# RMS norm with swish on one core: register work gathered at the top of the loops, a scratch transfer left out, and three loads cut in two

## The chip, the cores and the metric

The kernel runs on one core of a Trainium2 chip. The metric is the device time of one execution in microseconds. Before the change it is 160.35 us, the median of three runs (160.17 to 160.7).

## The reference

The input x is 16 x 1024 rows of 512 float32 numbers (33.55 MB), gamma has 512 numbers and eps is 1e-5. Every row is normalised by its own root mean square, multiplied by gamma and put through swish:

```python
rms = np.sqrt(np.mean(x ** 2, axis=-1, keepdims=True) + eps)
x_norm = x / rms * gamma
return x_norm * (1.0 / (1.0 + np.exp(-x_norm)))
```

The output has the same shape and type as x, so 33.55 MB are read from HBM and 33.55 MB are written.

## The kernel before

**Tiling.** The 16384 rows are spread over 128 partitions, 128 rows to a partition. A "row" below is one such index: 128 rows of x at once, one on each partition, 2 KB on each, 256 KB together. The rows lie in four groups (32, 48, 16 and 32 of them); within a group each partition's rows are contiguous in HBM, so a transfer of n rows is one run of n x 2 KB on each partition. In SBUF they lie in `xb`, a ring of 96 places, worked on in place; row 96 takes the place of row 0.

**Transfers.** All large transfers are issued by SP, into one queue, in the order of the list `order` (lines 33 to 36). `loads` (line 30) cuts the 128 rows into 11 loads and `stores` (line 32) into 6 stores. SP first issues the loads up to row 79. It then waits until the load of rows 48 to 74 has landed, waits for the first 8 units and issues the store of rows 0 to 31 ("store 0"), the load of rows 80 to 95, waits until store 0 is done (its ring places are then free), issues the loads of rows 96 to 121 and 122 to 127, waits until the first of these two has landed, and issues the other five stores, each when the rows that it covers are finished (`s_swish`, line 122). The first two loads (`early = 2`) are put into the entry block ahead of SP's first drain (lines 145 to 154), so that they go out before the barrier with which the program begins. At the end SP waits for the scratch transfer (line 164) and for the stores.

**Compute.** Work goes in units of `cn = 4` rows, 32 units in all. For a unit, ACT squares three of the rows and sums them (`square`, line 206), DVE does the fourth (`sums`, line 244), POOL adds eps and takes the power -0.5 (`rsqrt`, line 182), DVE multiplies the four rows by that and by gamma (`norm`, line 251), and ACT applies Silu to the unit's 2048 numbers per partition (`swish`, line 215). PE only waits for each load and raises `s_land` by the units that it completes. ACT begins with two units written out, then a loop of 10 rounds of three units, then two swishes; DVE and POOL have loops of the same ten rounds. In ACT's and DVE's loops the place in the ring is kept in registers, and every unit adds 4 to it, takes it modulo 96 and works out an address for each row that it touches (lines 235 to 240 and 272 to 277, with `rows_of` and `row_of`).

**Small transfers.** ACT's queue carries two: `scratch`, 128 x 16 zeros written from SBUF to an HBM tensor that nothing reads (line 219), and gamma, read to four partitions (line 223) and spread by DVE to all.

Of the kernel before, what the change touches and what calls it, by code (L numbers as in the profile page):

```python
# [9 lines left out]
def kernel(  # L10
# [7 lines left out]
    nc = tc.nc  # L18
    P = nc.NUM_PARTITIONS
    AF = mybir.ActivationFunctionType  # L20
    ALU = mybir.AluOpType
    fp32 = mybir.dt.float32

    xf = x.flatten_outer_dims()
    of = out.flatten_outer_dims()
    R, D = xf.shape

    groups = [32, 48, 16, 32]
    ring = 96
    loads = [(0, 4), (4, 4), (8, 8), (16, 8), (24, 8), (32, 16), (48, 27), (75, 5)]  # L30
    loads += [(80, 16), (96, 26), (122, 6)]
    stores = [(0, 32), (32, 32), (64, 16), (80, 16), (96, 24), (120, 8)]
    order = [("load", a) for a in (0, 4, 8, 16, 24, 32, 48, 75)]
    order += [("landed", 48), ("store", 0), ("load", 80)]
    order += [("stored", 0), ("load", 96), ("load", 122)]
    order += [("landed", 96)] + [("store", a) for a in (32, 64, 80, 96, 120)]
    early = 2
    cn = 4

# [11 lines left out]
    U = 3  # L51
    rounds = (K - 2) // U
    assert U * rounds == K - 2
    load_at = {a: t for t, (a, _) in enumerate(loads)}
# [9 lines left out]
    def sbuf(name, shape, dt=fp32):  # L64
        return nc.alloc_sbuf_tensor(name, shape, dt).ap()

    xb = sbuf("xb", [P, ring, D])
# [9 lines left out]

    ld = [nc.alloc_semaphore(f"ld{t}") for t in range(len(loads))]
    st = [nc.alloc_semaphore(f"st{t}") for t in range(len(stores))]
    scratch = nc.dram_tensor("scratch", [P, 16], fp32, kind="Internal").ap()  # L80
    blank = sbuf("blank", [P, 16])
    s_blank = nc.alloc_semaphore("s_blank")
    s_scratch = nc.alloc_semaphore("s_scratch")
    s_gld = nc.alloc_semaphore("s_gld")
    s_zero = nc.alloc_semaphore("s_zero")
    s_half = nc.alloc_semaphore("s_half")
# [1 line left out]
    s_land = nc.alloc_semaphore("s_land")  # L88
# [7 lines left out]
    def need(ins, sem, value):  # L96
        return ins.wait_op(sem, value, "sem-ge")

    def take(queue, sem):
        queue.wait_ge(sem, 1).then_inc(sem, -1)  # L100

    def dram(ap, piece):
        a, n = piece
        g = max(g for g in range(len(groups)) if first[g] <= a)
        r = a - first[g]
        assert r + n <= groups[g], piece
        rows = ap[P * first[g] : P * (first[g] + groups[g])]
        return rows.rearrange("(p n) d -> p n d", n=groups[g])[:, r : r + n, :]

    def buf(piece):  # L110
        a, n = piece
        at = a % ring
        assert at + n <= ring, piece
        return xb[:, at : at + n, :]

    def load(t):
        return nc.sync.dma_start(
            out=buf(loads[t]), in_=dram(xf, loads[t])
        ).then_inc(ld[t], 16)

    def store(t):
        need(
            nc.sync.dma_start(out=dram(of, stores[t]), in_=buf(stores[t])),
            s_swish, ends[t],
        ).then_inc(st[t], 16)
# [17 lines left out]
    entry = nc.main_func.blocks[0].instructions  # L143
    here = nc.cur_bb.bb.instructions
    for t in range(early):
        ins = load(t).ins
        assert here[-1] is ins or here[-1].name == ins.name
        here.pop()
        at = next(
            i for i, other in enumerate(entry)  # L150
            if other.engine == mybir.EngineType.SP
            and isinstance(other, mybir.InstDrain)
        )
        entry.insert(at, ins)
    for what, a in order[early:]:
        if what == "load":
            load(load_at[a])
        elif what == "store":
            store(store_at[a])
        elif what == "landed":  # L160
            nc.sync.wait_ge(ld[load_at[a]], 16)
        else:
            nc.sync.wait_ge(st[store_at[a]], 16)
    nc.sync.wait_ge(s_scratch, 16)
    waited = {a for what, a in order if what == "stored"}
    for t, (a, _) in enumerate(stores):
        if a not in waited:
# [2 lines left out]
    passed = 0  # L170
    for t, (a, n) in enumerate(loads):
        units = (a + n) // cn
        nc.tensor.wait_ge(ld[t], 16).then_inc(s_land, units - passed)
        passed = units
    assert passed == K

    nc.gpsimd.memset(blank, 0.0).then_inc(s_blank, 1)  # L177
    nc.gpsimd.memset(gamma4, 0.0).then_inc(s_zero, 1)  # L178
    nc.gpsimd.memset(neg_half, -0.5).then_inc(s_half, 1)  # L179
    nc.gpsimd.wait_ge(s_half, 1)  # L180
# [14 lines left out]
        for j in range(U):  # L195
            rsqrt((2 + j) % U)

    def rows_of(queue, v, j, n=1):
        return xb[:, bass.ds(queue.snap(v + j, min_val=0, max_val=ring - n), n), :]

    def row_of(queue, v, j):
        if isinstance(v, int):
            return xb[:, v + j, :]
        return rows_of(queue, v, j).rearrange("p n d -> p (n d)")

    def square(u, rows):
        take(nc.scalar, s_land)
        for j in range(cn - 1):
            acc = nc.scalar.activation(  # L209
                out=junk[u * (cn - 1) + j], in_=rows[j], func=AF.Square,  # L210
                scale=inv_d**0.5, accum_out=ms[u][:, j : j + 1],
            )
        acc.then_inc(s_acc, 1)

    def swish(rows):
        take(nc.scalar, s_norm)
        nc.scalar.activation(out=rows, in_=rows, func=AF.Silu).then_inc(s_swish, 1)  # L217

    need(nc.scalar.dma_start(out=scratch, in_=blank), s_blank, 1).then_inc(
        s_scratch, 16  # L220
    )
    need(
        nc.scalar.dma_start(out=gamma4[0:P:32, :], in_=gamma.partition_broadcast(4)),
        s_zero, 1,
    ).then_inc(s_gld, 16)
    nc.scalar.preload_act_table_set("silu_and_others")  # L226
    at = [nc.scalar.alloc_register(f"at{j}") for j in range(U)]
    nc.scalar.reg_mov(at[1], 0)
    nc.scalar.reg_mov(at[2], cn)
    for k in range(2):  # L230
        square(k, [xb[:, k * cn + j, :] for j in range(cn)])
    with nc.scalar.Fori(0, rounds, 1):
        for j in range(U):
            now, old = at[j], at[(j + 1) % U]
            nc.scalar.reg_alu(now, at[(j + 2) % U], cn, op=ALU.add)
            nc.scalar.reg_alu(now, now, ring, op=ALU.mod)
            v = nc.scalar.snap(now, min_val=0, max_val=ring - cn)
            square((2 + j) % U, [row_of(nc.scalar, v, i) for i in range(cn)])
            w = nc.scalar.snap(old, min_val=0, max_val=ring - cn)
            swish(xb[:, bass.ds(w, cn), :])  # L240
    for k in range(K - 2, K):
        swish(buf((k * cn, cn)))

    def sums(u, row):
        take(nc.vector, s_acc)
        nc.vector.scalar_tensor_tensor(  # L246
            out=junk_v[u], in0=row, scalar=inv_d, in1=row,
            op0=ALU.mult, op1=ALU.mult, accum_out=ms[u][:, cn - 1 : cn],
        ).then_inc(s_sum, 1)

    def norm(u, rows):
        take(nc.vector, s_rstd)
        for j in range(cn):
            ins = nc.vector.scalar_tensor_tensor(  # L254
                out=rows[j], in0=rows[j], scalar=rstd[u][:, j : j + 1],
                in1=gamma_sb, op0=ALU.mult, op1=ALU.mult,
            )
        ins.then_inc(s_norm, 1)

    to = [nc.vector.alloc_register(f"to{j}") for j in range(U)]  # L260
    nc.vector.reg_mov(to[2], cn)
    sums(0, xb[:, cn - 1, :])
    need(nc.vector.stream_shuffle(gamma_sb, gamma4, [0] * 32), s_gld, 16).then_inc(  # L263
        s_gamma, 1
# [1 line left out]
    sums(1, xb[:, 2 * cn - 1, :])  # L266
    nc.vector.wait_ge(s_gamma, 1)
    norm(0, [xb[:, j, :] for j in range(cn)])
    with nc.vector.Fori(0, rounds, 1):
        for j in range(U):  # L270
            now, old = to[j], to[(j + 2) % U]
            nc.vector.reg_alu(now, old, cn, op=ALU.add)
            nc.vector.reg_alu(now, now, ring, op=ALU.mod)
            v = nc.vector.snap(now, min_val=0, max_val=ring - cn)
            sums((2 + j) % U, row_of(nc.vector, v, cn - 1))
            w = nc.vector.snap(old, min_val=0, max_val=ring - cn)
            norm((1 + j) % U, [row_of(nc.vector, w, i) for i in range(cn)])
    norm((K - 1) % U, [buf(((K - 1) * cn + j, 1))[:, 0, :] for j in range(cn)])


# [33 lines left out]
```

## Time and profile before

| | before |
|---|---|
| median of 3 runs | 160.35 us (160.17 to 160.7) |
| the profiled execution's own time | 159.91 us |
| its span | 158.6 us |
| bytes moved | 67.14 MB, 423 GB/s over the span |
| DMA queue q1 (SP's transfers) | 98.7% of 16 engines' span |
| ACT, DVE, POOL busy | 121.1, 107.9, 59.3 us |
| last store issued | 133.5 us |

The profile shows one execution. Its shares are busy time over the span. The DMA rows count packets, megabytes and the packets' time as a share of sixteen DMA engines over the span; a share can pass 100% in a short window, because a packet's time is counted where it starts. q1 is SP's queue, q10 ACT's, q14 carries instructions. In the rows of windows the columns are the stretch, its length, busy time of DVE, ACT and POOL with instruction counts, the clock of TensorE (not used here), the DMA engines' share and GB/s. The trace also records for each DMA packet its queue, start, duration and bytes, but not its engine. A transfer over 128 partitions is 128 packets, eight for each engine, and each engine ends its part with a 4-byte packet, called a completion mark here; the wait for a transfer ends when all sixteen are there. Packets of one engine follow each other so closely that they can be laid end to end, and in that way followed by engine.

### The profile page before, as it was taken

To read this page: it belongs to the slowest core of one execution; us is meant where nothing else is said; L and a number is where in the kernel's file an instruction comes from. 1 tells how busy PE (TensorE), PEld (TensorE's weight loads), DVE (VectorE), ACT (ScalarE), POOL (GpSimd) and SP (SyncE) were. 2 spreads that over 40 slices of the span, in tenths; PEclk is the share of its full clock that TensorE was granted. 3 is DMA by queue.
4 is the path that set the end of the run, shared out by engine and by line. 5 is a ranking of instruction groups with operands and counts; after the bars stand their busy time and mean duration, and the time that the engine had idled before them with its cause. 6 is when DMAs were issued, how large, how long until landed. Compare 5 with 4: busy or idle time off the path is not lost. (4 is left out here: it accounts for less than half of the span.)

```text
span 158.6 us, 1330 instructions
## 1 busy us (share of the span) xinstructions
DVE 107.9 (68%) x194; ACT 121.1 (76%) x225; POOL 59.3 (37%) x71
## 2 busy tenths in 40 slices
DVE  0119798888888888888888887989898991000000
ACT  0836999999999999999999999999999954000000
POOL 2034445555455555554444444444454530000000
DMA  7999999999969969979999999996989999999976
GB/s 267 433 428 438 430 481 432 482 446 432 446 300 546 496 298 512 463 314 421 405 430 430 430 430 410 516 512 281 529 380 405 405 504 405 479 397 397 508 343 273
DMA packets 2602, 67.14 MB, mean 423 GB/s; under 512 B 420, under 2 KB 420, under 8 KB 424
## 3 DMA queue, kind: packets, MB, share of 16 engines
q1 hardware_dynamic: 2448, 67.11, 98.7%
q10 hardware_dynamic: 152, 0.02, 0.1%
q14 instruction: 2, 0.02, 0.0%
HBM read 33.56 MB, written 33.56 MB: 423 GB/s over the span
## 5 line engine op out<-in xcount | busy, mean ns | idle before, releaser
L254 DVE SCALAR_TENSOR_TENSOR xb<-xb,rstd,gamma_sb 128x512 f32 (+1 forms) x128 | 87.5, 747 | 0.1
L217 ACT ACTIVATE xb<-xb (+1 forms) x32 | 61.1, 1908 | 4.8 <-ACTq L100 4.2
L209 ACT ACTIVATE junk<-xb 128x512 f32 (+1 forms) x96 | 56.1, 585 | 4.0 <-ACTq L100 3.9
L188 POOL TENSOR_TENSOR rstd<-aeps,neg_half 128x4 f32<-128x4 f32 x32 | 40.9, 1279 | 5.9 <-POOLq L100 5.9
L184 POOL TENSOR_SCALAR aeps<-ms 128x4 f32<-128x4 f32 x32 | 17.6, 550 | 61.5 <-POOLq L100 61.5
L246 DVE SCALAR_TENSOR_TENSOR junk_v<-xb 128x512 f32 (+1 forms) x32 | 22.1, 692 | 20.1 <-DVEq L100 20.1
L209 ACT ACTIVATION_READ_ACCUMULATOR junk<-xb 128x1 f32 x96 | 17.9, 186 | 0.0
L226 ACT ACT_TABLE_LOAD x1 | 1.3, 1283 | 3.7 <-issue 3.7
L246 DVE DVE_READ_ACCUMULATOR junk_v<-xb 128x1 f32 x32 | 2.7, 83 | 0.0
L263 DVE LOAD_MASK_SELECT gamma_sb<-gamma x1 | 0.0, 14 | 3.4 <-DMA gamma<-in_gamma_dram 3.4
L263 DVE STREAM_SHUFFLE gamma_sb<-gamma 128x512 f32<-128x512 f32 x1 | 0.7, 719 | 0.0
L177 POOL MEMSET blank<- 128x16 f32 x1 | 0.1, 111 | 1.5 <-POOLq L62 1.5
L178 POOL MEMSET gamma<- 128x512 f32 x1 | 0.5, 524 | 0.0
L295 POOL MEMSET const-float32-0.0<- 128x1 f32 x1 | 0.1, 98 | 0.2 <-issue 0.2
L295 POOL MEMSET const-uint8-127<- 128x1 uint8 x1 | 0.1, 103 | 0.0
L295 POOL MEMSET const-bfloat16-1.0<- 128x1 bf16 x1 | 0.1, 101 | 0.0
L179 POOL MEMSET neg_half<- 128x4 f32 x1 | 0.1, 101 | 0.0
L295 POOL MEMSET const-float32-1.0<- 128x1 f32 x1 | 0.1, 98 | 0.0
## 6 DMA issues: line engine op xcount, KB each, us to landing
xb<-in_x_dram SPq DMA_DIRECT2D x2, 4096.0 KB, 30.4
out_dram<-xb SPq DMA_DIRECT2D x2, 4096.0 KB, 33.5
xb<-in_x_dram SPq DMA_DIRECT2D x1, 6912.0 KB, 44.7
xb<-in_x_dram SPq DMA_DIRECT2D x1, 6656.0 KB, 25.4
xb<-in_x_dram SPq DMA_DIRECT2D x3, 2048.0 KB, 14.7
out_dram<-xb SPq DMA_DIRECT2D x1, 6144.0 KB, 26.4
xb<-in_x_dram SPq DMA_DIRECT2D x2, 1024.0 KB, 5.8
out_dram<-xb SPq DMA_DIRECT2D x1, 2048.0 KB, 25.0
```

What stands on the lines that cost most here:

```text
L177: nc.gpsimd.memset(blank, 0.0).then_inc(s_blank, 1)
L178: nc.gpsimd.memset(gamma4, 0.0).then_inc(s_zero, 1)
L179: nc.gpsimd.memset(neg_half, -0.5).then_inc(s_half, 1)
L184: nc.gpsimd.tensor_scalar(out=aeps[u], in0=ms[u], scalar1=eps_f, scalar2=None, op0=ALU.add,).then_inc(s_eps, 1)
L188: nc.gpsimd.tensor_tensor(out=rstd[u], in0=aeps[u], in1=neg_half, op=ALU.pow).then_inc(s_rstd, 1)
L209: acc = nc.scalar.activation(out=junk[u * (cn - 1) + j], in_=rows[j], func=AF.Square, scale=inv_d**0.5, accum_out=ms[u][:, j : j + 1],)
L217: nc.scalar.activation(out=rows, in_=rows, func=AF.Silu).then_inc(s_swish, 1)
L226: nc.scalar.preload_act_table_set("silu_and_others")
L246: nc.vector.scalar_tensor_tensor(out=junk_v[u], in0=row, scalar=inv_d, in1=row, op0=ALU.mult, op1=ALU.mult, accum_out=ms[u][:, cn - 1 : cn ...
L254: ins = nc.vector.scalar_tensor_tensor(out=rows[j], in0=rows[j], scalar=rstd[u][:, j : j + 1], in1=gamma_sb, op0=ALU.mult, op1=ALU.mult,)
L263: need(nc.vector.stream_shuffle(gamma_sb, gamma4, [0] * 32), s_gld, 16).then_inc(s_gamma, 1)
L295: nc = _bacc.Bacc("TRN2", target_bir_lowering=False, num_devices=1)
```

## The change

- ACT's and DVE's loops count units instead of rounds. At the top of each round `addresses` works out the addresses that the round needs (twelve on ACT, thirteen on DVE) from the loop's counter; the registers for the place in the ring, with their additions, modulos and copies per unit, are gone.
- The scratch transfer, the memset of its source, its two semaphores and SP's final wait are gone.
- The load of rows 48 to 74 becomes two, of 16 and 11 rows; the load of rows 96 to 121 becomes two, of 16 and 10. The two waits for a landed load now name the second pieces (rows 64 and 112).
- The first load (rows 0 to 3) goes out as two transfers on one semaphore: partitions 0 to 15, then 16 to 127. Both, and the second load, lie in the entry block ahead of SP's first drain.

```diff
-    loads = [(0, 4), (4, 4), (8, 8), (16, 8), (24, 8), (32, 16), (48, 27), (75, 5)]
-    loads += [(80, 16), (96, 26), (122, 6)]
+    loads = [(0, 4), (4, 4), (8, 8), (16, 8), (24, 8), (32, 16), (48, 16), (64, 11), (75, 5)]
+    loads += [(80, 16), (96, 16), (112, 10), (122, 6)]
-    order = [("load", a) for a in (0, 4, 8, 16, 24, 32, 48, 75)]
-    order += [("landed", 48), ("store", 0), ("load", 80)]
-    order += [("stored", 0), ("load", 96), ("load", 122)]
-    order += [("landed", 96)] + [("store", a) for a in (32, 64, 80, 96, 120)]
+    order = [("load", a) for a in (0, 4, 8, 16, 24, 32, 48, 64, 75)]
+    order += [("landed", 64), ("store", 0), ("load", 80)]
+    order += [("stored", 0), ("load", 96), ("load", 112), ("load", 122)]
+    order += [("landed", 112)] + [("store", a) for a in (32, 64, 80, 96, 120)]
...
+    parts = [[slice(0, P)] for _ in loads]
+    parts[0] = [slice(0, 16), slice(16, P)]
+    full = [16 * len(p) for p in parts]
+
     def load(t):
-        return nc.sync.dma_start(
-            out=buf(loads[t]), in_=dram(xf, loads[t])
-        ).then_inc(ld[t], 16)
+        return [
+            nc.sync.dma_start(
+                out=buf(loads[t])[part], in_=dram(xf, loads[t])[part]
+            ).then_inc(ld[t], 16)
+            for part in parts[t]
+        ]
...
-    nc.sync.wait_ge(s_scratch, 16)
...
-    nc.gpsimd.memset(blank, 0.0).then_inc(s_blank, 1)
...
+    slots = ring // cn
+    units = xb.rearrange("p (u n) d -> p u (n d)", n=cn)
+
+    def unit_of(i):
+        return units[:, bass.ds(i % slots, 1), :].rearrange("p u e -> p (u e)")
+
+    def row_of(unit, r):
+        return unit[:, r * D : (r + 1) * D]
+
+    def addresses(queue, aps):
+        for ap in aps:
+            queue.lower_ap(ap)
...
-    need(nc.scalar.dma_start(out=scratch, in_=blank), s_blank, 1).then_inc(
-        s_scratch, 16
-    )
...
-    with nc.scalar.Fori(0, rounds, 1):
+    with nc.scalar.Fori(0, rounds * U, U) as i:
+        new = [unit_of(i + j + 2) for j in range(U)]
+        old = [unit_of(i), unit_of(i + 1), new[0]]
+        sq_rows = [[row_of(unit, r) for r in range(cn - 1)] for unit in new]
+        addresses(nc.scalar, old + sum(sq_rows, []))
         for j in range(U):
-            now, old = at[j], at[(j + 1) % U]
-            nc.scalar.reg_alu(now, at[(j + 2) % U], cn, op=ALU.add)
-            nc.scalar.reg_alu(now, now, ring, op=ALU.mod)
-            v = nc.scalar.snap(now, min_val=0, max_val=ring - cn)
-            square((2 + j) % U, [row_of(nc.scalar, v, i) for i in range(cn)])
-            w = nc.scalar.snap(old, min_val=0, max_val=ring - cn)
-            swish(xb[:, bass.ds(w, cn), :])
+            square((2 + j) % U, sq_rows[j])
+            swish(old[j])
...
-    with nc.vector.Fori(0, rounds, 1):
+    with nc.vector.Fori(0, rounds * U, U) as i:
+        of_unit = [unit_of(i + j + 1) for j in range(U + 1)]
+        rows = [[row_of(unit, r) for r in range(cn)] for unit in of_unit]
+        addresses(nc.vector, sum(rows[:U], []) + rows[U][cn - 1 :])
         for j in range(U):
-            now, old = to[j], to[(j + 2) % U]
-            nc.vector.reg_alu(now, old, cn, op=ALU.add)
-            nc.vector.reg_alu(now, now, ring, op=ALU.mod)
-            v = nc.vector.snap(now, min_val=0, max_val=ring - cn)
-            sums((2 + j) % U, row_of(nc.vector, v, cn - 1))
-            w = nc.vector.snap(old, min_val=0, max_val=ring - cn)
-            norm((1 + j) % U, [row_of(nc.vector, w, i) for i in range(cn)])
+            sums((2 + j) % U, rows[j + 1][cn - 1])
+            norm((1 + j) % U, rows[j])
```

More of the change, by code (lines that the diff above doesn't have):

```diff
@@ L79 @@
     st = [nc.alloc_semaphore(f"st{t}") for t in range(len(stores))]
[L80 to L83, printed above, removed]
     s_gld = nc.alloc_semaphore("s_gld")
@@ L145 @@
     for t in range(early):
-        ins = load(t).ins
-        assert here[-1] is ins or here[-1].name == ins.name
-        here.pop()
+        moved = [piece.ins for piece in load(t)]
+        for ins in reversed(moved):
+            assert here[-1] is ins or here[-1].name == ins.name
+            here.pop()
         at = next(
@@ L153 @@
         )
-        entry.insert(at, ins)
+        for ins in reversed(moved):
+            entry.insert(at, ins)
     for what, a in order[early:]:
@@ L160 @@
         elif what == "landed":
-            nc.sync.wait_ge(ld[load_at[a]], 16)
+            nc.sync.wait_ge(ld[load_at[a]], full[load_at[a]])
         else:
             nc.sync.wait_ge(st[store_at[a]], 16)
-    nc.sync.wait_ge(s_scratch, 16)
     waited = {a for what, a in order if what == "stored"}
@@ L172 @@
         units = (a + n) // cn
-        nc.tensor.wait_ge(ld[t], 16).then_inc(s_land, units - passed)
+        nc.tensor.wait_ge(ld[t], full[t]).then_inc(s_land, units - passed)
         passed = units
     assert passed == K
-    nc.gpsimd.memset(blank, 0.0).then_inc(s_blank, 1)
     nc.gpsimd.memset(gamma4, 0.0).then_inc(s_zero, 1)
@@ L196 @@
             rsqrt((2 + j) % U)
[L198 to L204, printed above, removed]
+    slots = ring // cn
[7 more added lines that the diff above has]
+            queue.lower_ap(ap)
     def square(u, rows):
@@ L226 @@
     nc.scalar.preload_act_table_set("silu_and_others")
-    at = [nc.scalar.alloc_register(f"at{j}") for j in range(U)]
-    nc.scalar.reg_mov(at[1], 0)
-    nc.scalar.reg_mov(at[2], cn)
     for k in range(2):
         square(k, [xb[:, k * cn + j, :] for j in range(cn)])
-    with nc.scalar.Fori(0, rounds, 1):
-        for j in range(U):
-            now, old = at[j], at[(j + 1) % U]
-            nc.scalar.reg_alu(now, at[(j + 2) % U], cn, op=ALU.add)
-            nc.scalar.reg_alu(now, now, ring, op=ALU.mod)
-            v = nc.scalar.snap(now, min_val=0, max_val=ring - cn)
-            square((2 + j) % U, [row_of(nc.scalar, v, i) for i in range(cn)])
-            w = nc.scalar.snap(old, min_val=0, max_val=ring - cn)
-            swish(xb[:, bass.ds(w, cn), :])
+    with nc.scalar.Fori(0, rounds * U, U) as i:
[3 more added lines that the diff above has]
+        addresses(nc.scalar, old + sum(sq_rows, []))
+        for j in range(U):
+            square((2 + j) % U, sq_rows[j])
+            swish(old[j])
     for k in range(K - 2, K):
-        swish(buf((k * cn, cn)))
+        swish(units[:, k % slots, :])
     def sums(u, row):
@@ L258, in norm @@
         ins.then_inc(s_norm, 1)
-    to = [nc.vector.alloc_register(f"to{j}") for j in range(U)]
-    nc.vector.reg_mov(to[2], cn)
     sums(0, xb[:, cn - 1, :])
```

## The prediction

> **What bounds the kernel now.** I read the page's shares first, then the DMA queues, then SP's waits, then the DMA in narrow windows.
>
> ```profile
> span 158.6 us, 1330 instructions
> DVE 107.9 (68%) x194; ACT 121.1 (76%) x225; POOL 59.3 (37%) x71
> DMA  7999999999969969979999999996989999999976
> q1 hardware_dynamic: 2448, 67.11, 98.7%
> q10 hardware_dynamic: 152, 0.02, 0.1%
> q14 instruction: 2, 0.02, 0.0%
> ```
>
> The reader is to see a DMA-bound kernel: SP's queue (q1) fills 98.7% of what sixteen DMA engines have, and no compute engine passes 76%. q14 counts two packets of instructions; they matter below.
>
> ```profile
> SPq L161 <- DMA xb<-in_x_dram: 68.4, 2, 43.8
> SPq L123 <- ACT xb L217: 35.3, 3, 22.3
> SPq L117 <- DMA out_dram<-xb: 21.6, 1, 21.6
> ```
>
> These are SP's own waits, for landed loads, for finished swishes and for the one store that frees ring rows. They would cost time only if the DMA engines ran dry. In the packet records (start, duration, bytes of each) they never do: laid end to end the packets make sixteen unbroken rows from 1.04 to 158.07 us, with no gap above 0.13 us other than two of 0.30 us named below. Compute ends at 133.5 us and the stores then drain until 158, so compute is about 20 us off the path.
>
> ```profile
> 0.00:1.00 1.00, 0.00 (x0) 0.00 (x0) 0.19 (x4) 1.00 0.00 0
> 1.00:1.40 0.40, 0.00 (x0) 0.00 (x0) 0.00 (x0) 1.00 1.47 266
> 1.40:1.80 0.40, 0.00 (x0) 0.00 (x0) 0.00 (x0) 1.00 0.44 143
> 1.80:2.20 0.40, 0.00 (x0) 0.00 (x0) 0.28 (x2) 1.00 0.88 348
> 3.00:4.00 1.00, 0.00 (x0) 0.33 (x1) 0.00 (x0) 1.00 0.98 410
> ```
>
> Windows at the start (last column GB/s): nothing moves for 1.0 us, and full rate comes only after 2 us. Then the DMA view of two windows, 22 to 23 us and 157 us to the end:
>
> ```profile
> q1 hardware_dynamic: 16, 0.52, 123.3%
> q14 instruction: 1, 0.01, 1.9%
> ```
>
> and
>
> ```profile
> DMA packets 18, 0.03 MB, mean 21 GB/s; under 512 B 16, under 2 KB 16, under 8 KB 16
> ```
>
> The second says that in the last 1.6 us only two data packets start; the other sixteen are the completion marks. So the tail is two engines alone: fourteen write their mark at 157.15 to 157.57 us, two at 158.02 and 158.07. Who is late can be followed back by the marks at the end of every transfer. Until 21 us all sixteen stand within 0.5 us. An 8192-byte q14 packet runs at 22.44 and another at 27.33 us, each on an engine whose neighbouring q1 packets show a gap of 0.30 us and a packet longer by 0.31 and 0.61 us. At 31 us two engines are late, one by about 0.4, one by about 0.75 us; they end at 157.57 and 158.03. The third, ending at 158.07, is another kind: its 64 KB store packets take 2.45 to 2.52 us where the rest take 2.418, and it loses about 0.7 us between 101 and 128 us, none after compute stops.
>
> The profiled execution took 159.91 us, span 158.6 and 1.31 around it, 0.44 under the median of 160.35. I work the sum as a difference and apply it to the median.
>
> **The change part by part.**
>
> *Shorter loop programs.* Each round of ACT and DVE now has about 53 instructions, 25 (ACT) and 28 (DVE) of them register work (ACT's FUSED_REGOPS alone are x90 on line 209 in ten rounds). The new loops work out 12 (ACT) and 13 (DVE) addresses once at the top; the per-unit add, modulo and copies go. With 12 or 13 address instructions and a few modulos in place of some 25 to 28, I estimate 10 to 14 instructions fewer per loop. On the engines that is worth nothing: register work runs ahead while the 1.91 us swish or the 2.65 us of norms execute. The new block costs 12 x 60 ns = 0.72 us on ACT and 13 x 69 = 0.90 on DVE, under those covers. If the cover failed wholly, ten rounds would lose about 9 us, and the last 8 rows' store, issued at 133.5, is first touched by a DMA engine at 153.2: still hidden.
>
> What a shorter program can move is the fetch: if it no longer asks for the two 8192-byte packets, the engines ending at 158.03 and 157.57 fall back to the others at 157.46. The term is 158.07 - 157.46 = 0.6 us at most, and 0 if the fetch remains or if the engine with the long store packets still ends at 158.07. Its loss goes with running instructions, of which there are fewer. I take -0.5, nearer to the full end, because two late engines of three are the fetch's.
>
> [...]
>
> *No scratch transfer.* 128 packets of 64 B at 11 ns, 8 per engine, plus a completion mark: 8 x 11 + 9 = 0.10 us per engine between 5.5 and 9.3 us. The transfer that runs through them took 4.90 us by its marks, the next of the same size 4.86. Between 0.04 and 0.10 saved; I take 0.05, the marks being the nearer row. The memset on POOL (0.11) and the issue on ACT (0.36) go at a place where ACT's first square waits for load 0 and the table load (4.96): nothing. SP's final wait for it ended long before.
>
> *Later loads cut in two.* Rows 48 to 74 go as 16 + 11, rows 96 to 121 as 16 + 10. A 32768-byte packet takes 1.213 us and 16384 takes 0.611, so a packet costs about 8 ns beside its bytes. Eight more per engine and a mark is 8 x 6 + 6 = 0.055 us each time, measured against 2.041 and 1.966 for the long packets: +0.11 for both. The landed wait moves to the second piece, which ends the same bytes; behind it on SP stand store 0 and everything later. Store 0 is issued at 48.79 and its first packet starts at 50.10, when the five rows behind are through: 1.3 us of cover, against 1.04 from the first issue to the first packet. It is the thinnest cover in the kernel; gone, it costs its deficit on all engines. An engine no longer late shortens the landed wait and widens it. Two more issues cost SP 0.33 to 0.45 us each, the first before 5.5 us with work queued to 47, the second at 71.6 with load 80 queued to 79.5: nothing.
>
> *First load in two.* Now: issue 0 to 0.383, first packets at 1.04 to 1.80 over the engines, first packets taking 0.42 to 0.99 where 0.309 is the steady value, marks at 3.90 to 4.38. The 16-partition piece gives every engine one packet, perhaps sooner; the other seven come with an issue 0.33 to 0.43 us later. The best end is that all start with the earliest: the mean start is about 1.25, so -0.2. The worst is that an engine finishes its packet before the next is there and pays the first-packet excess (0.1 to 0.68) again: +0.5. I take -0.1, since first packets now end at 1.65 to 2.2 and the second piece's should be there from 1.5 to 2.2. The extra issue also moves the start barrier by 0.43 us; loads 2 to 7 are then issued from 2.35, and the first engine needs load 2 at 6.39: nothing.
>
> [...] No row here shows a load cut by partitions. [...]
>
> *Sum:* -0.5 - 0.05 + 0.11 - 0.1 = -0.54; 160.35 - 0.54 = 159.8 us.
>
> **The rivals.**
>
> (a) *The fetch stays, or the third late engine hides its loss.* [...] Then -0.05 + 0.11 with the start between -0.2 and +0.2: 160.2 to 160.6, no change.
>
> (b) *The start runs dry, slower.* Place: each engine between its one packet of piece one and the first of piece two. Price: the first-packet excess, +0.3 to +0.6 on all engines, decisive when piece two's packets come after 2.2 us and the fetch stays. For it: the issues are 0.43 apart and late engines start at 1.75 and 1.80 today, so theirs would come at about 2.2. Against: the other engines have 0.2 us or more in hand. With +0.06 from the rest: 160.7 to 161.0.
>
> (c) *Store 0 comes late*, from the thinnest cover: +0.1 to +0.3, 160.5 to 160.7. Against: that cover rather grows.
>
> **How the numbers follow.** About 0.3% (0.48 us) is what a measurement here can tell from no change. Fetch gone and seen in the time: 0.42, 159.3 to 159.85. Rival (a): 0.35, of which a part touches the lower bound. Rival (b): 0.15 and (c) with other late or cold transfers 0.08; most of both lie over 160.83, and I leave 0.22 to slower, 0.36 to no change. The range from 159.3 to 160.9 leaves out a start that gains and the fetch together, and the upper half of (b). The forecast's own range is 159.3 to 159.9.
>
> **What would show it.** Right: no q14 packet inside the span, the last sixteen marks within about 0.45 us, no q10 packets of 64 B, the first mark of load 0 before 3.9 us. Wrong: q14 still there; a gap between the first and second packet of an engine before 2.5 us; a DMA dip at 48 to 51 us; or a tail carried by the engine with the long store packets.

## The result and the profile after

The change made the kernel slower: 161.65 us median of 6 runs (161.39 to 161.78) against 160.33 us median of 6 (160.17 to 160.7). The ratio on record is 1.0069 with a 95% interval from 1.005 to 1.0089; the ratios below are those on record too, and can differ a little from the quotient of two medians (1.0082 here). The time lies above the range that was given.

The lines of the page after that answer to those shown of before:

```profile
span 160.2 us, 990 instructions
DVE 107.9 (67%) x194; ACT 119.9 (75%) x225; POOL 59.2 (37%) x70
q1 hardware_dynamic: 2752, 67.11, 98.5%
q10 hardware_dynamic: 8, 0.01, 0.0%
q14 instruction: 1, 0.01, 0.0%
```

The kernel is still bound by its DMA engines; compute did not become slower, and 340 instruction records fewer are there: the loops are shorter as the diff says, by some 16 (ACT) and 18 (DVE) in a round. The scratch transfer is gone from q10. One of the two instruction packets is left inside the span. SP's waits, the second view shown of before, hardly moved:

```profile
SPq L166 <- DMA xb<-in_x_dram: 67.8, 2, 43.6
SPq L126 <- ACT xb L225: 33.8, 3, 21.8
SPq L118 <- DMA out_dram<-xb: 22.1, 1, 22.1
```

The start is where the time went. The windows of the kernel after (stretch, length, busy DVE, ACT and POOL, clock, DMA share, GB/s):

```profile
1.00:1.40 0.40, 0.00 (x0) 0.00 (x0) 0.00 (x0) 1.00 1.22 328
1.40:1.80 0.40, 0.00 (x0) 0.00 (x0) 0.00 (x0) 1.00 1.97 266
1.80:2.20 0.40, 0.00 (x0) 0.00 (x0) 0.00 (x0) 1.00 0.24 61
2.20:2.60 0.40, 0.00 (x0) 0.00 (x0) 0.21 (x1) 1.00 0.44 164
2.60:3.00 0.40, 0.00 (x0) 0.00 (x0) 0.35 (x2) 1.00 0.98 389
3.00:4.00 1.00, 0.00 (x0) 0.00 (x0) 0.00 (x0) 1.00 1.11 360
4.00:5.00 1.00, 0.00 (x0) 0.92 (x1) 0.00 (x0) 1.00 0.99 287
5.00:6.00 1.00, 0.00 (x0) 0.37 (x1) 0.00 (x0) 1.00 0.95 320
```

and two windows of before that were not shown yet:

```profile
4.00:5.00 1.00, 0.00 (x0) 0.99 (x2) 0.00 (x0) 1.00 1.04 434
5.00:6.00 1.00, 0.00 (x0) 1.00 (x3) 0.00 (x0) 1.00 0.97 403
```

The first packets do come a little faster (328 GB/s against 266 in the first window). But then the rate falls to 61 and 164 GB/s until 2.6 us, and from 3 to 6 us it is 287 to 360 GB/s where before had 403 to 434. The DMA share is near 1 there: the engines are not idle, their packets take longer. In the packet records the marks of load 1 (rows 4 to 7) come at 7.53 to 7.90 us; before they came at 6.39 to 6.87. Both kernels give every engine sixteen packets of 8192 bytes for loads 0 and 1. Their durations add up to 5.38 us per engine before and 6.53 after, 1.15 more, and of these 0.34 fall on the first two packets of an engine and nearly all the rest on the eight that follow. Of the first two, the packet of the 16-partition piece takes 0.49 us (mean; before's first packet 0.66) and the first packet of the 112-partition piece 0.87 (before's second 0.35). Five engines also stand idle between these two, for 0.05 to 0.52 us; over all sixteen that is under 0.1 us per engine, and the first packets start 0.13 us earlier on the mean (1.13 in place of 1.26).

The profiled executions took 159.91 and 161.78 us, 1.87 apart. Fourteen engines write their last mark at 157.15 to 157.57 us before and at 158.03 to 158.52 after: 0.9 of the start's loss is still there. The last mark of all moved by more, from 158.07 to 159.67, since one engine is now 1.1 us behind the fourteen where the last was 0.5 behind: 0.6 to 0.7 more. The remaining 0.3 lies outside the span (1.31 and 1.58). The DMA view of the window from 158.6 us to the end, and of 135 to 136 us, after:

```profile
DMA packets 3, 0.02 MB, mean 10 GB/s; under 512 B 2, under 2 KB 2, under 8 KB 2
```

and

```profile
q14 instruction: 1, 0.01, 1.9%
```

One data packet starts in the last 1.6 us: a single engine carries the end. It is the one whose store packets are long; it loses again in the stores, and is 0.95 us behind the others at 119 us, 1.1 at 129. The instruction packet now runs at 135.45 us, and its engine ends at 158.95. It was moved, not removed.

### The profile page after: what moved, and what is told of

Same layout as the page of the kernel before. It is cut to its first block, busy times and chain, and to the rows that moved or that the text cites. A ratio compares the mean times of both kernels' runs of the same rounds, so it can differ in the third digit from the quotient of the medians.

```text
span 160.2 us, 990 instructions
## 1 busy us (share of the span) xinstructions
DVE 107.9 (67%) x194; ACT 119.9 (75%) x225; POOL 59.2 (37%) x70
## 3 DMA queue, kind: packets, MB, share of 16 engines
q1 hardware_dynamic: 2752, 67.11, 98.5%
```

## The experiments

Each kernel is compared with before on the same chip. Before's median was 160.38, 160.43, 160.77 and 160.61 us in the four sets of runs.

**Is it the cut of the first load?** Two kernels: the changed one with the first load whole (its edit is shown), and the one before with that cut alone.

```diff
-    parts[0] = [slice(0, 16), slice(16, P)]
```

> The changed kernel with its first load as one transfer again; all else of the change stays. Theory A (the cut of the first load costs the time, about 1.1 us by the marks of load 1): 160.4 to 160.7 us, marks of load 0 back at 3.9 to 4.4 us. Rival (the loss lies in the shorter loops or in the later cuts): 161.5 us, as the changed kernel.

> The kernel before with nothing but its first load cut in two, partitions 0 to 15 and 16 to 127. Theory A: 161.3 to 161.5 us, marks of load 0 at 4.7 to 5.2 us. Rival: 160.3 us.

The first measured 160.47 us, a ratio of 1.0011 (0.9995 to 1.0027); the second 161.51 us, 1.0067 (1.0048 to 1.0085). The whole loss of the change comes and goes with these two transfers. The windows of the kernel with the first load whole:

```profile
3.00:4.00 1.00, 0.00 (x0) 0.39 (x1) 0.00 (x0) 1.00 1.05 442
4.00:5.00 1.00, 0.00 (x0) 0.90 (x1) 0.00 (x0) 1.00 0.98 410
5.00:6.00 1.00, 0.00 (x0) 0.95 (x3) 0.00 (x0) 1.00 1.00 418
```

and of the one with nothing but the cut:

```profile
3.00:4.00 1.00, 0.00 (x0) 0.00 (x0) 0.00 (x0) 1.00 1.05 360
4.00:5.00 1.00, 0.00 (x0) 0.86 (x1) 0.00 (x0) 1.00 1.00 295
5.00:6.00 1.00, 0.00 (x0) 0.43 (x1) 0.00 (x0) 1.00 0.92 320
```

**Do the engines run dry, or are the pieces slow?** First the order of the pieces was turned, then the cut was put into load 1, where the engines have work queued.

```diff
-    parts[0] = [slice(0, 16), slice(16, P)]
+    parts[0] = [slice(0, 112), slice(112, P)]
```

> The changed kernel, but its first load is cut as partitions 0 to 111 first, then 112 to 127: seven packets for each engine, so no engine can be done with them before the second piece's single packet is there. Theory D (the engines run dry after one packet and pay the first-packet excess again): 160.5 us, no second set of first packets over 0.6 us. Theory M (112 partitions dealt seven to an engine are read more slowly, 0.42 us a packet where 0.309 is steady): 161.1 to 161.3 us, with load 0's later packets at 0.40 to 0.45 us.

```diff
-    parts[0] = [slice(0, 16), slice(16, P)]
+    parts[1] = [slice(0, 16), slice(16, P)]
```

> The changed kernel with its first load whole and the second load (rows 4 to 7) cut instead, 16 and 112 partitions; the first load keeps the engines busy until 3.9 us, so nothing can run dry. Theory D: as with the first load whole, 160.4 to 160.7 us, load 1's packets at 0.309 to 0.32 us. Theory M: 0.5 to 0.8 us more than that, with load 1's packets at 0.40 to 0.45 us.

They measured 161.94 us (ratio 1.0097, 1.0076 to 1.0117) and 162.28 us (1.0118, 1.0096 to 1.014). Both cost more than the change itself, though in both the engines have other packets queued while the second piece is issued (the DMA share from 1 to 4 us is 0.95 to 1.04). Windows of the second:

```profile
4.00:5.00 1.00, 0.00 (x0) 0.92 (x1) 0.00 (x0) 1.00 1.32 279
5.00:6.00 1.00, 0.00 (x0) 0.36 (x1) 0.00 (x0) 1.00 0.76 188
6.00:7.00 1.00, 0.00 (x0) 0.89 (x3) 0.00 (x0) 1.00 0.95 295
7.00:8.00 1.00, 0.00 (x0) 1.00 (x4) 0.00 (x0) 1.00 1.16 320
```

Load 1 here has packets of some 0.8 us right behind the 16-partition piece, and of 0.41 to 0.50 further on in the 112-partition one. Running dry falls as the main cause, and with it the mechanism of rival (b): slow packets alone cost as much and more. The loss was over what theory M had named; the small piece and the packets right behind it are slow too, which it had not priced.

**Which partitions, or which part of HBM?** In these three the first load is whole, and load 1 is changed: once in contiguous halves, once in even and odd partitions, and once whole, with the rows of partition p + 16 read into partition p.

```diff
+    parts[1] = [slice(0, 64), slice(64, P)]
```

> The changed kernel with its first load whole and the second load (rows 4 to 7) cut into partitions 0 to 63 and 64 to 127, four packets for each engine in each piece. Theory M (an engine is slow on partitions that are not the eight it has in a whole transfer, because several engines then share what leads to the same partitions): 1 to 2.5 us over the same kernel uncut (160.47), 161.5 to 163 us, load 1's packets at 0.4 to 0.6 us. Rival N (any transfer on fewer than 128 partitions, or any extra transfer, costs a fixed amount): as the even and odd cut, whatever that gives.

```diff
+    parts[1] = [slice(0, P, 2), slice(1, P, 2)]
```

> [...] Theory M: no loss, 160.4 to 160.6 us, load 1's packets at 0.309 to 0.32 us. Rival N: as the halves.

```diff
+        rows = xf[16 * 32 : (16 + P) * 32].rearrange("(p n) d -> p n d", n=32)
+        return rows[:, 4:8, :]
```

> [...] Theory M on the SBUF side: no loss, 160.4 to 160.6 us. Rival H (the loss comes from the HBM side, an engine that reads where its neighbour read): load 1's packets at 0.4 us or more and 161 us or more.

The halves took 162.84 us (1.0143, 1.0111 to 1.0174), the even and odd cut 160.27 us (0.9983, 0.9965 to 1.0), the other rows 160.56 us (1.0007, 0.9987 to 1.0027). Window from 5 to 7 us of the halves:

```profile
5.00:6.00 1.00, 0.00 (x0) 0.99 (x2) 0.00 (x0) 1.00 0.95 197
6.00:7.00 1.00, 0.00 (x0) 1.00 (x3) 0.00 (x0) 1.00 1.01 238
```

of the even and odd cut:

```profile
5.00:6.00 1.00, 0.00 (x0) 0.99 (x2) 0.00 (x0) 1.00 0.98 410
6.00:7.00 1.00, 0.00 (x0) 1.00 (x3) 0.00 (x0) 1.00 1.14 475
```

and of the other rows:

```profile
5.00:6.00 1.00, 0.00 (x0) 0.95 (x3) 0.00 (x0) 1.00 0.98 410
```

This is the clearest reading of the study. Two transfers of 64 partitions each, equal in bytes, packets and issue, differ by a factor of two in rate: in the halves a packet takes about 0.6 us, in the even and odd cut 0.309. All that differs in the edit is which partitions a transfer holds. The rows of partition p + 16, read into partition p, cost nothing (1.0007, and 410 GB/s from 5 to 6 us), which points to the side of SBUF; that is argued, not shown. A half also reads from a narrower stretch of HBM, 4 MB in place of 8, and no run was made for that alone; but the load of rows 80 to 95 lies within 4 MB too, and its 32 KB packets took 1.213 us (median, before), the same as those of rows 32 to 47 (12 MB). That several engines share what leads to the same partitions is the explanation that theory M gives; its numbers for the halves came true (162.84 us, 0.6 us a packet), but no run shows the sharing.

**How slow is a 16-partition piece, and do two transfers cost by themselves?** Load 1 in eight pieces of 16 neighbours, with the first load whole; the first load cut into even and odd partitions; the first load cut by rows.

```diff
+    parts[1] = [slice(q, q + 16) for q in range(0, P, 16)]
```

> The changed kernel with its first load whole and the second load (rows 4 to 7) cut into eight transfers of 16 neighbouring partitions, one packet for each engine in each. [...] If neighbouring eights of partitions share one way (as the halves alone would also allow), eight packets share and load 1 takes about 20 us: 178 us. If only the number of transfers costs: 160.5 to 162 us.

```diff
-    parts[0] = [slice(0, 16), slice(16, P)]
+    parts[0] = [slice(0, P, 2), slice(1, P, 2)]
```

> [...] Theory M (what costs is which partitions an engine is dealt, not that there are two transfers): 160.3 to 160.7 us, as with the first load whole. Theory D (a second transfer at the start pays the first-packet excess again): 161 us, with a second set of packets over 0.6 us at 2.2 to 2.6 us.

```diff
-    parts[0] = [slice(0, 16), slice(16, P)]
+    parts[0] = [(slice(0, P), slice(0, 2)), (slice(0, P), slice(2, 4))]
```

> The changed kernel with its first load cut by rows (rows 0 and 1, then 2 and 3), all 128 partitions in both transfers. Theory M (the partitions of a piece are what costs): 160.3 to 160.6 us, marks of load 1 at 6.4 to 7.0 us as with the first load whole. Theory D (a second transfer at the start costs by itself): 161 us or more, marks of load 1 at 7 us or more.

The eight pieces took 164.81 us (1.0262, 1.0228 to 1.0296). Its windows:

```profile
5.00:6.00 1.00, 0.00 (x0) 0.00 (x0) 0.56 (x2) 1.00 0.94 131
6.00:7.00 1.00, 0.00 (x0) 0.12 (x1) 0.00 (x0) 1.00 1.00 139
7.00:8.00 1.00, 0.00 (x0) 1.00 (x1) 0.00 (x0) 1.00 1.00 139
```

A packet settles at 0.914 us, 2.96 times 0.309: 131 KB in 0.915 us, about 143 GB/s. Neither expectation hit it: by sharing among eight a packet would take 2.5 us (8 x 0.309, an estimate), and by the number of transfers alone the kernel would take 162 us at most. The completion marks of one piece are spread over 0.9 us, as long as a piece takes, so two neighbouring pieces run beside each other, and 0.914 us need not be the price of one by itself. For the change it is enough that sixteen neighbours take three times their time at full rate.

The first load in even and odd partitions took 161.63 us (1.0054, 1.0033 to 1.0075), cut by rows 160.52 us (1.0009, 0.9987 to 1.0031). The cut by rows is the cleaner one: two transfers at the start, all partitions in both, and no loss that can be measured against the first load whole (1.0011). Its marks of load 1 came late, though, at 6.82 to 7.51 us, 0.4 to 0.5 later than expected, so some tenths at the start do go to the second transfer in that execution and are not seen in the medians. The even and odd cut has another trouble: SP needed 0.545 us for its first issue in place of 0.383, and the first packet started at 1.33 us in place of 1.02; one engine also had a single packet of 1.43 us and stayed behind to the end. A second set of long first packets, which theory D wanted, is not there (one packet of sixteen over 0.6 us), and nearly all packets of both pieces and of load 1 take 0.309 us. Set against the profile with the first load whole, the middle engine (the median of a transfer's sixteen marks) is 0.46 us late at load 1 and still 0.48 at the load of rows 75 to 79, and 1.22 at the load of rows 122 to 127. Most of the difference comes where the DMA engines turn from store 0 to loads and back. Whether the cut brings that about is open, so this kernel neither bears the account out nor refutes it. With the 0.5 us that the cut by rows loses in its marks it leaves room for a few tenths, of the change's 1.1 at the start, that belong to any second transfer there.

**What are the other parts worth?** The loops, the missing scratch transfer and the later cuts, with the first load whole, in all combinations (the one with all three is the first experiment). Of each edit the line that names it is shown, and the lines that go with it are left out.

```diff
-    scratch = nc.dram_tensor("scratch", [P, 16], fp32, kind="Internal").ap()
```

> The kernel before without the scratch transfer, nothing else. Loops and scratch together, without the later cuts, measured 161.13 us, 0.7 us over before. If leaving out the scratch transfer costs it: 161.0 to 161.2 us here. If the shorter loops cost it: 160.3 to 160.4 us. By the term of the prediction: 160.35 us.

```diff
-    with nc.scalar.Fori(0, rounds, 1):
+    with nc.scalar.Fori(0, rounds * U, U) as i:
```

> The kernel before with the shorter loops only; the scratch transfer stays, the later loads are uncut. If the shorter loops cost the 0.7 us: 161.0 to 161.2 us. If the scratch transfer's absence does: 160.3 to 160.5 us. By the prediction's term for the fetch: 159.9 us.

```diff
-    loads = [(0, 4), (4, 4), (8, 8), (16, 8), (24, 8), (32, 16), (48, 27), (75, 5)]
+    loads = [(0, 4), (4, 4), (8, 8), (16, 8), (24, 8), (32, 16), (48, 16), (64, 11), (75, 5)]
```

> The kernel before with the two later loads cut, nothing else. By the prediction 0.11 us slower: 160.5 us. By the difference of the two kernels with the first load whole (160.47 with the cuts, 161.13 without) the cuts are worth 0.6 us: 159.8 us. If they only undo a skew that the other parts bring: 160.3 to 160.5 us.

Two of the parts together: the first and the second of these edits, the second and the third, the first and the third.

```diff
-    scratch = nc.dram_tensor("scratch", [P, 16], fp32, kind="Internal").ap()
...
+    with nc.scalar.Fori(0, rounds * U, U) as i:
```

> The changed kernel with its first load whole and the two later loads uncut: only the shorter loops and the missing scratch transfer stay. By the terms of the prediction 0.11 us less than with the later cuts: 160.35 us; with the fetch's two packets gone from the loads and no longer on the last engine 159.8 us. Rival (the long-store engine ends last whatever the fetch does, so loops and scratch are worth nothing): 160.3 to 160.5 us.

```diff
+    with nc.scalar.Fori(0, rounds * U, U) as i:
...
+    loads = [(0, 4), (4, 4), (8, 8), (16, 8), (24, 8), (32, 16), (48, 16), (64, 11), (75, 5)]
```

> The kernel before with the shorter loops and the two later cuts; scratch transfer kept, first load whole. If the parts add up (loops 0.9984, cuts 0.9991 of before): 0.9975 of before, 159.9 to 160.1 us. If none of them is worth anything: the same as before within 0.2%.

```diff
-    scratch = nc.dram_tensor("scratch", [P, 16], fp32, kind="Internal").ap()
...
+    loads = [(0, 4), (4, 4), (8, 8), (16, 8), (24, 8), (32, 16), (48, 16), (64, 11), (75, 5)]
```

> The kernel before without the scratch transfer and with the two later cuts; long loops, first load whole. If the missing scratch transfer costs (1.0012 alone): 1.0003 of before with the cuts added. If none is worth anything: the same as before within 0.2%.

| parts in place, first load whole | median us | ratio to before | 95% interval |
|---|---|---|---|
| no scratch | 160.82 | 1.0012 | 0.9992 to 1.0031 |
| loops | 160.35 | 0.9984 | 0.9961 to 1.0007 |
| cuts | 160.47 | 0.9991 | 0.9971 to 1.0011 |
| loops, no scratch | 161.13 | 1.0029 | 1.0013 to 1.0046 |
| loops, cuts | 160.82 | 1.0018 | 0.9998 to 1.0039 |
| no scratch, cuts | 160.58 | 1.0015 | 0.9993 to 1.0036 |
| all three | 160.47 | 1.0011 | 0.9995 to 1.0027 |

Six of the seven cannot be told from before. Loops without the scratch transfer and without cuts stand out at 0.3%, above all three times that were expected of them. In that kernel's trace two engines fall behind where the DMA engines turn from store 0 to loads and back: behind the load of rows 122 to 127 fourteen write their marks at 98.9 to 99.8 us, two at 101.2 and 101.4. The same place costs between 0.22 and 1.0 us per engine from profile to profile (packet time over the usual, 66 to 102 us), also in kernels with a ratio near 1. Why this one combination is hit, when each part alone is not and all three together are not, stays open.

The loops' kernels agree on the fetch. The page of the kernel with the loops alone:

```profile
q14 instruction: 1, 0.01, 0.0%
```

In every profile with the shorter loops one packet runs between 131 and 140 us and the other after the last store; in every one with the long loops both run between 22 and 29. So the fetch depends on the loops, as predicted. It is put off until after ACT and DVE leave their loops (in the changed kernel their last branches run at 124.7 and 125.2 us, the packet at 135.45). In the changed kernel its engine ends late all the same, at 158.95 us; with the first load whole it ends at 157.48, level with the others, and the engine with the long store packets ends last, at 158.05.

## Why the prediction was wrong, point by point

*What bounds the kernel* was right: DMA time alone counts (q1 fills 98.5% of the span after, 98.7% before), and most of the loss at the start was carried to the end, 0.9 of 1.15 us on fourteen engines.

*First load in two* is the step that failed. It was given -0.1 us, with +0.5 as the worst; the cut is worth 161.65 against 160.47 us, +1.2, and 161.51 against 160.38, +1.1, when made alone. The part of it that came true is small: the first packets start at 1.03 to 1.33 us over the engines, before at 1.04 to 1.80. The step counted packets per engine and the time of issue and asked nothing of which partitions a piece has. The row that no trace of before could give, a transfer over a part of the partitions, was bounded by first-packet times, which is another thing. The measured prices are 0.915 us for a packet of sixteen neighbours and 0.41 to 0.50 for a packet of the 112, both in place of 0.309. By these the one and the seven packets would cost about 0.6 and 0.7 to 1.3 us. The 1.15 that were measured are made up otherwise: the one packet is 0.18 us shorter than before's first, the first of the seven 0.52 longer, the other six 0.5 together, and the first two of load 1, right behind them, 0.27.

*Rival (b)* had the right side, with 0.15, but for the most part the wrong mechanism and place. The gap that it names is there on five engines, and with the long first packets of the second piece it makes some 0.3 us of the loss at the start; the other 0.8 lie on the eight packets behind, which follow each other without a gap.

*Shorter loops:* that the register work was hidden is right. Of the fetch, -0.5 failed, the second term of the sum that did: loops alone 0.9984 with 1 inside the interval, and with all but the cut of the first load in place 160.47 us, where the sum without that cut gives 159.9. The term assumed that the two packets go; they were put off. It also chose the larger end although the profile shown had a third engine that ended last for another reason; that engine ended last after the change, too. This was rival (a), and it holds for all but the first load.

*No scratch transfer*, -0.05, and *later cuts*, +0.11: both too small to be seen, as measured (1.0012 and 0.9991, both intervals with 1 inside). The second was worked out with 6 ns a packet where the sentence before has 8. The packets with the first load whole give more: 1.213 + 0.762 us for 16 and 10 rows against 1.966 for 26, and 1.213 + 0.841 for 16 and 11 against 2.041 for 27, so 9 and 13 ns, and about +0.19 with the marks. *Store 0's cover* held: its issue came at 49.38 us with work queued until 51.5.

*Signs:* of those named for being wrong, three came: an instruction packet inside the span, a gap between the first two packets of some engines before 2.5 us, and a tail carried by the engine with the long store packets. The dip at 48 to 51 us did not.

## What to carry to other kernels

If a transfer has to be cut, cut it by rows and not into runs of neighbouring partitions: 64 neighbours ran at half the rate here (0.6 us a packet in place of 0.309), 16 at a third (0.914). Even and odd partitions cost nothing in load 1 (0.9983), but as the first load they cost about as much as the change (1.0054 against 1.0069), for a reason that is not known. In a kernel bound by DMA a term for a new shape of transfer needs a row of that shape; packet counts are not enough. Before a late engine is priced, look at which engine would be last without it.

## What the runs showed of the hardware

- A transfer of 1 MB in neighbouring halves cost 2.4 us more than whole (162.84 against 160.47), in even and odd partitions nothing (160.27), though both are two transfers of 64 partitions.
- Packets right behind a 16-partition piece are slow too: in the kernel with the 112-partition piece first, the first packets of the whole load 1 took some 0.8 us there, in place of 0.309.
- A transfer over 64 partitions, neighbours or every second one, took SP 0.53 to 0.59 us to issue; ahead of the barrier at the start one over 128, 112 or 16 partitions took 0.38 to 0.46. Right behind two of 64 partitions, though, one over 128 took 0.585.
- One DMA engine has longer 64 KB store packets (2.44 to 2.52 us, the median of all 2.418), in before and after, all between 50 and 121 us, while compute runs (until 133.5 and 133.2 us), and ends last in both (158.07 and 159.67 us). Its cause was not tried.
